# The products for v in blocks of 256 features over both halves of a third, with their split weights kept in DRAM

## The chip, the cores and the metric

The kernel runs on one core of a Trainium2 chip. The metric is the device time of one execution in microseconds (us), as the median of several runs. Five engines work beside each other, each through its own queue in program order: PE (TensorE, whose weight loads are listed apart as PEld), DVE (VectorE), ACT (ScalarE), POOL (GpSimd) and SP (SyncE), which issues nearly all DMA transfers here.

## The reference

One layer of a bidirectional encoder trunk on 1024 + 2048 positions of width 1024, all in float32. The change touches only the columns `v_a` of the input projection, which go through GELU and a layer norm over their 1024 features before the position mixing:

```python
h = rmsnorm(x, norm_g[i])
proj = h @ w_in[i]
u_a, v_a, z_a, x_b, z_b = jnp.split(proj, splits, axis=-1)
y_a = gmlp_branch(gelu(u_a), gelu(v_a), z_a, ...)   # u * (w_s mixes layernorm(v)) * silu(z)
y_b = s5_branch(x_b, z_b, ...)                      # two scans, GELU, GLU, silu(z)
x = x + jnp.concatenate([y_a, y_b], axis=-1) @ w_out[i]
return rmsnorm(x, final_g)
```

## The kernel before

**Split products.** Every float32 operand of a big product is held as two float32r parts, hi (index 0) and lo (index 1), and a product is three matmuls: hi by hi, hi by lo, lo by hi (`mm3`, L57 to L61). A weight piece of 1024 x 128 or 256 x 512 values is a tile `whl` (two parts, 1 MB together). `stage_next` lets SP load it from the input as two tiles `wf` of 128 x 512 (L107), of which there is one buffer each; `split_w` then makes hi on ACT (`S.copy`, L151) and lo on POOL (`G.tensor_tensor`, L152). Of `whl` there are two buffers. `next_w` does one `split_w` and one `stage_next`, after a sweep or part has used a tile.

**Thirds and stages.** The 3072 rows are three thirds, each of two halves (`jh`) of 512 rows, each half of four chunks of 128 rows. A half's normalised and transposed input is eight tiles `ha0..7` or `hb0..7` (two parts, 128 features x 512 rows). Phase one makes x_b for all thirds (0 to 398 us). Phase two (398 to 1824 us) takes the thirds in the order 2, 0, 1; each has a **v stage**, a **z stage** (zb, with the position mixing `mix`, whose products go to tiles `sv`) and a **u stage** (u and za). In z and u a weight piece is the stationary operand of 24 matmuls for each half, 48 in all (`sweep`). The last phase does the GLU and the output projection.

**The v stage.** Here the chunk of h is stationary and 512 features of the weights stream. The loops run over `jh`, two blocks `cb` of 512 features and four quarters `q` of the 1024 inputs: 16 weight pieces in a third, each used for one half only, in 24 matmuls (L494 to L496, four chunks, each with a PSUM bank `acc`). At the last quarter ACT applies GELU (L499). After the first half `half_stats(0)` takes bn_stats, bn_aggr and an inverse square root by Newton steps (`newton_rsqrt`, L48 to L53) on DVE, and `norm_chunk` and `split_chunk` prepare the first chunk for `mix`.

**Kept weights.** In the first third run, the split tiles of z, u and za (24) are also written to DRAM (`wc_d`, L154); the other two thirds read them back ready-made (L146), without ACT and POOL. The v pieces are loaded and split anew in each third.

**Side work.** `advance` is called at the same points as `next_w` and a few more; it advances 64 groups of state-space scans (`s5_groups`) through phase two: matmuls `pb` and `py`, and on DVE a chain of products, two scans and products (L1068 to L1086). Names of S5 tiles are `b`, `h`, `u`, `gt`, `tab`. For the second and third third `get_half` loads the tiles `ha`, `hb` back from DRAM (`hf<-hs_d`, L417) through the two buffers of `stage_tile` and splits them (L421 on ACT, L422 on POOL and DVE by turns). The scheduler orders each engine's instructions by the priorities given (`tc.high_priority`).

Of the kernel before, what the change touches and what calls it, by code (L numbers as in the profile page):

```python
# [11 lines left out]
F32 = mybir.dt.float32  # L12
# [3 lines left out]
AF = mybir.ActivationFunctionType  # L16
# [5 lines left out]
P = 128  # L22
D = 1024
KT = 8
# [7 lines left out]
HP = 100  # L32
# [31 lines left out]
def hybrid_encoder(ctx, tc, a, outs):  # L64
# [19 lines left out]
    wc_d = dram.tile([3 * KT, P, 2 * KT * P], F32, name="wc_d")  # L84
# [30 lines left out]
    def load_wv(col, q):  # L115

        src = w_in[256 * q:256 * q + 256, col:col + 512].rearrange("(kt p) c -> p kt c", p=P)
        return ([stage_w(i, src[:, i:i + 1]) for i in range(2)],
                lambda w: w.rearrange("p s (t a) c -> p s t (a c)", t=2))
# [6 lines left out]
    for i in range(NTH):  # L126
        order += [(None, load_wv, D + 512 * cb, q) for _ in range(2) for cb in range(2) for q in range(4)]
        feats = [4 * D + P * fb for fb in range(KT)] + [2 * D * z + P * fb for fb in range(KT) for z in range(2)]
        order += [(n, load_w, f) if i == 0 else (n,) for n, f in enumerate(feats)]
# [233 lines left out]
    with ExitStack() as p2:  # L363
# [64 lines left out]
        for th in (2, 0, 1):  # L428
# [3 lines left out]
            lns = {}  # L432

            def half_stats(jh):

                with tc.high_priority(offset=HP):
                    mv = small.tile([P, 4, 2], F32, tag="mv", name="mv")
                    for c in range(4):
                        st = small.tile([P, 2, 6], F32, tag="st", name="st")
                        for i in range(2):  # L440
                            V.bn_stats(st[:, i], vs[jh][:, c, 512 * i:512 * i + 512])
                        V.bn_aggr(mv[:, c], st)
                    ve = small.tile([P, 4], F32, tag="ve", name="ve")
                    V.tensor_scalar(ve, mv[:, :, 1], EPS, None, op0=ALU.add)
                    rs = newton_rsqrt(nc, small, ve, 4, "rv")
                    nb = small.tile([P, 4], F32, tag="nb", name="nb")
# [37 lines left out]
            for jh in range(2):  # L484
                for cb in range(2):
                    acc = [ps_mm.tile([P, 512], F32, tag="mm", name="acc") for _ in range(4)]
                    for q in range(4):
                        w = ready.pop(0)
                        for c in range(4):
                            csl = slice(P * c, P * c + P)  # L490
                            for i in range(2):
                                h = hs[jh][2 * q + i]
                                first, last = q == 0 and i == 0, q == 3 and i == 1
# [648 lines left out]
```

## Time and profile before

| what | value |
|---|---|
| runs: median (lowest to highest of 3) | 2626.35 us (2624.52 to 2627.77) |
| profiled execution: own time / span of its trace | 2629.88 / 2628.0 us |
| mean granted clock of PE in the profile | 0.979 |
| PE busy / PEld | 2472.4 us (94%) / 2033.7 us (77%) |
| DVE / ACT / POOL busy | 1812.0 (69%) / 1041.8 (40%) / 745.6 us (28%) |

Busy time is the union of an engine's instructions in the span. A matmul's listed length includes its way through the array, so what a matmul costs in a dense row is read from start to start. The granted clock is a share of full speed: 1.0 is 2.4 GHz and 0.5 is 1.2 GHz.

### The profile page before, as it was taken

The page shows a single profiled execution, that of the slowest core. Times are in us where ns is not written, and L with a number is a line of the kernel's source. Part 1 is how long each engine was busy: PE and PEld are TensorE (multiplying, and loading weights), DVE is VectorE, ACT ScalarE, POOL GpSimd, SP SyncE. Part 2 cuts the span into 40 slices and gives each one's busy share as a digit, 9 for nine tenths or more (in the row PEclk, how much of TensorE's full clock was granted, in tenths as well). Part 3 has the DMA queues.
Part 4 walks back from the last instruction along what each step waited for, and adds up shares of the span by engine and source line. Part 5 has one row for each costly group of instructions (what it writes and reads, how often), then busy time and mean ns, then how long its engine had stood idle before and what let it go on. Part 6 is the DMA issues. An engine that isn't in the chain of part 4 may idle for free.

```text
span 2628.0 us, 32080 instructions
## 1 busy us (share of the span) xinstructions
PE 2472.4 (94%) x11161; PEld 2033.7 (77%) x11161; DVE 1812.0 (69%) x2890; ACT 1041.8 (40%) x1809; POOL 745.6 (28%) x703
## 2 busy tenths in 40 slices
PE   6899998898998789999988899999999999999998
PEld 5777786777877677888877778887888888888887
DVE  6897857898988898888888998883443443333332
ACT  5343344455445455554445545433232321111110
POOL 1579865544323463211135421101000100000000
PEclk9999998999999899999999999999999999999999
DMA  8565453344554534444444334445565642222221
GB/s 231 172 193 156 131 148 112 110 155 142 173 169 145 172 102 129 130 137 147 132 142 123 110 126 141 133 141 180 168 172 163 198 151 97 96 97 97 92 73 36
DMA packets 369028, 362.90 MB, mean 138 GB/s; under 512 B 41665, under 2 KB 305377, under 8 KB 359649
## 3 DMA queue, kind: packets, MB, share of 16 engines
q1 hardware_dynamic: 317024, 339.80, 41.3%
q10 hardware_dynamic: 51840, 21.04, 3.2%
q8 instruction: 88, 1.44, 0.2%
q14 instruction: 76, 0.61, 0.1%
HBM read 233.95 MB, written 126.81 MB: 137 GB/s over the span
## 4 chain that ended last, share of the span: by engine, by line
PE 44%; DVE 27%; issue 6%; ACT 6%; POOL 5%; DMA 4%; SPq 0%; ACTq 0%; POOLq 0%; DVEq 0%
PE mm L59 13%; PE mm L61 13%; PE mm L60 13%; DVE gt L1078 6%; POOL whl L152 2%; DVE h L1084 1%; DVE h L1083 1%; DVE b L1070 1%; DVE b L1069 1%; DVE h L1086 1%; DVE b L1071 1%; DVE tab L1028 1%; DVE u L1017 1%; DVE b L1068 1%; DVE v L543 1%
## 5 line engine op out<-in xcount | busy, mean ns | idle before, releaser
L152 POOL TENSOR_TENSOR whl<-wf,whl 128x512 fp32r<-128x512 f32 x192 | 295.8, 1558 | 300.4 <-ACT whl L151 274.9
L61 PE MATMUL mm<-w,yh 128*128 128x512 f32 x768 | 301.4, 393 | 0.0
L60 PE MATMUL mm<-w,yh 128*128 128x512 f32 x768 | 301.1, 392 | 0.0
L59 PE MATMUL mm<-w,yh 128*128 128x512 f32 x768 | 301.1, 392 | 0.0
L59 PE MATMUL mm<-ha,whl 128*128 128x512 f32 x704 | 282.3, 401 | 18.5 <-ACT whl L151 11.2
L61 PE MATMUL mm<-ha,whl 128*128 128x512 f32 x704 | 279.2, 397 | 2.3 <-POOL whl L152 2.1
L60 PE MATMUL mm<-ha,whl 128*128 128x512 f32 x704 | 279.0, 396 | 0.0
L59 PE MATMUL mm<-hb,whl 128*128 128x512 f32 x704 | 276.8, 393 | 0.0
L60 PE MATMUL mm<-hb,whl 128*128 128x512 f32 x704 | 275.0, 391 | 0.0
L61 PE MATMUL mm<-hb,whl 128*128 128x512 f32 x704 | 274.6, 390 | 0.0
L1078 DVE TENSOR_TENSOR_SCAN gt<-dec,b 64x768 f32<-64x768 f32 x128 | 239.5, 1871 | 3.7
L59 PEld LDWEIGHTS mm<-ha,whl 128*128 128x128 f32 x704 | 134.9, 192 | 47.6 <-ACT whl L151 12.6
L60 PEld LDWEIGHTS mm<-w,yh 128*128 128x128 f32 x768 | 144.2, 188 | 32.9
L59 PEld LDWEIGHTS mm<-w,yh 128*128 128x128 f32 x768 | 144.2, 188 | 32.6
L61 PEld LDWEIGHTS mm<-w,yh 128*128 128x128 f32 x768 | 144.1, 188 | 32.5
L1073 ACT ACTIVATE dec<-keep,r 128x768 f32<-128x768 f32 x64 | 60.1, 939 | 275.3 <-DVE gt L1078 275.3
L661 DVE SCALAR_TENSOR_TENSOR yh<-yf,yh 128x512 fp32r<-128x512 f32 x96 | 66.9, 699 | 146.4 <-ACT yh L660 109.2
L151 ACT CAST whl<-wf 128x512 fp32r<-128x512 f32 x192 | 112.5, 618 | 127.0 <-DMA wf<-in_w_in_dram 36.3
L61 PEld LDWEIGHTS mm<-ha,whl 128*128 128x128 f32 x704 | 134.8, 191 | 34.2 <-POOL whl L152 5.4
L690 DVE TENSOR_TENSOR xr<-xr,mm 128x512 f32<-128x512 f32 x48 | 33.0, 688 | 182.9 <-PE mm L61 182.9
L1017 POOL TENSOR_TENSOR mo<-m,mo 128x384 fp32r<-128x384 f32 x64 | 79.1, 1237 | 278.1 <-ACT mo L1016 265.4
L60 PEld LDWEIGHTS mm<-ha,whl 128*128 128x128 f32 x704 | 135.2, 192 | 26.7 <-DVE ha L285 0.4
(242 smaller groups left out, 5759.0 us busy)
## 6 DMA issues: line engine op xcount, KB each, us to landing
wf<-in_w_in_dram SPq DMA_DIRECT2D x192, 256.0 KB
whl<-wc_d SPq DMA_DIRECT2D x48, 1024.0 KB
wc_d<-whl SPq DMA_DIRECT2D x24, 1024.0 KB
m<-mat_d SPq DMA_DIRECT2D x128, 128.0 KB
xb_d<-xo SPq DMA_DIRECT2D x24, 512.0 KB
U<-xb_d SPq DMA_DIRECT2D x64, 192.0 KB
gy_d<-gy SPq DMA_DIRECT2D x64, 192.0 KB
zb_d<-zb SPq DMA_DIRECT2D x24, 512.0 KB
```

What stands on the lines that cost most here:

```text
L59: nc.tensor.matmul(out, lh, rh, start=first, stop=False)
L60: nc.tensor.matmul(out, lh, rl, start=False, stop=False)
L61: nc.tensor.matmul(out, ll, rh, start=False, stop=last)
L151: S.copy(flat[:, 0, sl], wf)
L152: G.tensor_tensor(flat[:, 1, sl], wf, flat[:, 0, sl].bitcast(F32), op=ALU.subtract)
L543: V.scalar_tensor_tensor(t, t, LG[:, fb:fb + 1], RB[:, fb:fb + 1].to_broadcast([P, 4, P]), op0=ALU.mult, op1=ALU.add)
L661: V.scalar_tensor_tensor(y[:, 1], yf, sc, y[:, 0].bitcast(F32), op0=ALU.mult, op1=ALU.subtract)
L690: V.tensor_tensor(x, x, t.ps[i], op=ALU.add)
L1017: eng.tensor_tensor(t[:, 1], src, t[:, 0].bitcast(F32), op=ALU.subtract)
L1028: V.scalar_tensor_tensor(fr, kio, f8l[:, g + q:g + q + 1], fr, op0=ALU.mult, op1=ALU.add)
L1073: S.activation(dec.rearrange("p (i k) -> p i k", i=2), keep.unsqueeze(1).to_broadcast(sh), AF.Copy, scale=r8[:, g:g + 1])
L1078: V.tensor_tensor_scan(o[r, f], dec[r, f], bf[r, f], 0.0, op0=ALU.mult, op1=ALU.add)
```

## The change

The v stage handles blocks of 256 features for both halves of a third. A weight piece is now 512 inputs x 256 features; a third has 8 instead of 16, each used for both halves, in 2 x 48 matmuls of 256 columns. Two chunks share a PSUM bank, so a block holds four banks for its eight chunks. Four parts `v_part` (half, input half `q`) make a block; the first block takes both of the first half's parts first. bn_stats is issued as soon as 512 features of a chunk are there. `half_stats(0)` and the first chunk's norm and split now stand before the last part of the last block. The v pieces, too, are written to `wc_d` in the first third run and read back in the others (8 + 24 tiles instead of 24).

```diff
-    wc_d = dram.tile([3 * KT, P, 2 * KT * P], F32, name="wc_d")
+    wc_d = dram.tile([4 * KT, P, 2 * KT * P], F32, name="wc_d")
...
     def load_wv(col, q):
 
-        src = w_in[256 * q:256 * q + 256, col:col + 512].rearrange("(kt p) c -> p kt c", p=P)
-        return ([stage_w(i, src[:, i:i + 1]) for i in range(2)],
-                lambda w: w.rearrange("p s (t a) c -> p s t (a c)", t=2))
+        src = w_in[512 * q:512 * q + 512, col:col + 256].rearrange("(kt p) c -> p kt c", p=P)
+        return [stage_w(i, src[:, 2 * i:2 * i + 2]) for i in range(2)], lambda w: w
...
-        order += [(None, load_wv, D + 512 * cb, q) for _ in range(2) for cb in range(2) for q in range(4)]
-        feats = [4 * D + P * fb for fb in range(KT)] + [2 * D * z + P * fb for fb in range(KT) for z in range(2)]
-        order += [(n, load_w, f) if i == 0 else (n,) for n, f in enumerate(feats)]
+        todo = [(load_wv, D + 256 * cb, q) for cb in range(4) for q in range(2)]
+        todo += [(load_w, 4 * D + P * fb) for fb in range(KT)]
+        todo += [(load_w, 2 * D * z + P * fb) for fb in range(KT) for z in range(2)]
+        order += [(n, *f) if i == 0 else (n,) for n, f in enumerate(todo)]
...
-            for jh in range(2):
-                for cb in range(2):
-                    acc = [ps_mm.tile([P, 512], F32, tag="mm", name="acc") for _ in range(4)]
-                    for q in range(4):
...
+            def v_part(acc, w, cb, q, jh):
+
+                for cc in range(2):
+                    ps = acc[jh][cc]
+                    for i in range(2):
+                        csl = slice(P * (2 * cc + i), P * (2 * cc + i) + P)
+                        for t in range(4):
+                            h, wh, wl = hs[jh][4 * q + t], w[:, 0, 2 * t:2 * t + 2], w[:, 1, 2 * t:2 * t + 2]
+
+                            mm3(nc, ps[:, i], h[:, 0, csl], h[:, 1, csl], wh, wl, q == t == i == 0, q == i == 1 and t == 3)
+                    if q:
+                        c = slice(2 * cc, 2 * cc + 2)
+                        sl = slice(256 * cb, 256 * cb + 256)
+                        with tc.high_priority(offset=HP):
+                            S.activation(vs[jh][:, c, sl], ps, AF.Gelu_apprx_tanh)
+                            for i in (2 * cc, 2 * cc + 1) if cb % 2 else ():
+                                V.bn_stats(sts[jh][:, i, cb // 2], vs[jh][:, i, 512 * (cb // 2):256 * cb + 256])
+                advance()
+
+            for cb in range(4):
+                acc = [[ps_mm.tile([P, 2, 256], F32, tag="mm", name="acc") for _ in range(2)] for _ in range(2)]
+                ws = [ready.pop(0) for _ in range(2)]
+
+                for jh, q in ((0, 0), (0, 1), (1, 0), (1, 1)) if cb == 0 else ((0, 0), (1, 0), (0, 1), (1, 1)):
+                    v_part(acc, ws[q], cb, q, jh)
+                    if jh:
+                        next_w()
+                    if cb == 3 and (jh, q) == (0, 1):
+                        half_stats(0)
+                        norm_chunk(0)
+                        split_chunk(0, 0)
+                        split_chunk(0, 1)
```

The new file's lines are 7 higher from `s5_groups` on (its L1068 is now L1075), and lines of the v stage moved by a few.

On PE, at the start of the second v stage, the rows before are these (`ha_8178`, `ha_8181` are the first two input tiles of the half):

```order
L494 MATMUL acc<-whl,ha_8178 128x512
L495 MATMUL acc<-whl,ha_8178 128x512
L496 MATMUL acc<-whl,ha_8178 128x512
L494 MATMUL acc<-whl,ha_8181 128x512
L495 MATMUL acc<-whl,ha_8181 128x512
L496 MATMUL acc<-whl,ha_8181 128x512
```

There they now are (`ha_8488` to `ha_8499` are the first four input tiles):

```order
L59 MATMUL acc<-whl,ha_8488 128x256
L60 MATMUL acc<-whl,ha_8488 128x256
L61 MATMUL acc<-whl,ha_8488 128x256
L59 MATMUL acc<-whl,ha_8491 128x256
L60 MATMUL acc<-whl,ha_8491 128x256
L61 MATMUL acc<-whl,ha_8491 128x256
L59 MATMUL acc<-whl,ha_8496 128x256
L60 MATMUL acc<-whl,ha_8496 128x256
L61 MATMUL acc<-whl,ha_8496 128x256
L59 MATMUL acc<-whl,ha_8499 128x256
L60 MATMUL acc<-whl,ha_8499 128x256
L61 MATMUL acc<-whl,ha_8499 128x256
```

The columns are halved, the count is doubled, and the first chunk already needs four input tiles instead of two.

On SP, where the second v stage begins, before (`hf` are the reloaded input tiles of the third, two feature blocks each; the first of the eight stands a few rows ahead; `wf` are v weights to be split; `ya_d<-za` is the last store of the third before):

```order
L417 DMA hf_8184<-hs_d 128x2x512
L107 DMA wf<-in_w_in_dram 128x512 x2
L417 DMA hf_8192<-hs_d 128x2x512
L417 DMA hf_8200<-hs_d 128x2x512
L515 DMA ya_d<-za 128x8x128
L107 DMA wf<-in_w_in_dram 128x512 x2
L1046 DMA m_8535<-mat_d 128x256
L417 DMA hf_8296<-hs_d 128x2x512
L417 DMA hf_8304<-hs_d 128x2x512
```

and now (`hf_8486` is the first of the eight):

```order
L417 DMA hf_8486<-hs_d 128x2x512
L1106 DMA gy_d<-gy 8x16x384
L1051 DMA m_8878<-mat_d 128x256
L1049 DMA U<-xb_d 128x1x384
L417 DMA hf_8494<-hs_d 128x2x512
L146 DMA whl<-wc_d 128x2048
L417 DMA hf_8502<-hs_d 128x2x512
L146 DMA whl<-wc_d 128x2048
L1053 DMA m_8880<-mat_d 128x256
L417 DMA hf_8510<-hs_d 128x2x512
L522 DMA ya_d<-za 128x8x128
L1055 DMA m_8880<-ks_d 128x1x128
```

The first two ready-made v tiles are read between the second, third and fourth input tile; the other four input tiles still follow the store.

On DVE, in the first third run, `half_stats(0)` ended like this before (the Newton steps L51 to L53 come three times; `v_4334` is v of the first half):

```order
L444 TENSOR_SCALAR ve<-mv 128x4
L48 TENSOR_SCALAR rvy<-ve 128x4
L51 TENSOR_TENSOR rva<-rvy 128x4
L52 SCALAR_TENSOR_TENSOR rva<-rva,ve 128x4
L53 SCALAR_TENSOR_TENSOR rvy<-rva,rvy 128x4
...
L447 SCALAR_TENSOR_TENSOR nb<-mv,rvy 128x4
L458 TENSOR_SCALAR v_4334<-v_4334,rvy,nb 128x1024 x4
```

and ends like this now (`v_4336` and `v_4337` are v of the first and second half):

```order
L53 SCALAR_TENSOR_TENSOR rvy<-rva,rvy 128x4
L498 BN_STATS st<-v_4337 128x6
L51 TENSOR_TENSOR rva<-rvy 128x4
L1086 MEMSET gt 64x2x2 x2
L52 SCALAR_TENSOR_TENSOR rva<-rva,ve 128x4
L440 BN_AGGR mv<-st 128x2
L1090 TENSOR_TENSOR h_5528<-gt,tab 128x768
L53 SCALAR_TENSOR_TENSOR rvy<-rva,rvy 128x4
L1091 TENSOR_TENSOR h_5529<-gt,tab 128x768
L445 SCALAR_TENSOR_TENSOR nb<-mv,rvy 128x4
L1024 TENSOR_TENSOR u<-U,u 128x384
L456 TENSOR_SCALAR v_4336<-v_4336,rvy,nb 128x1024
```

The small steps are now mixed with the second half's bn_stats and with one piece of an S5 group (L1075 to L1091 there, its two scans and its first four products included), and they stand at the end of the v stage instead of in its middle.

## Rows read from the trace of the kernel before

**Rows 1.** page, part 5: line, engine, op, tiles | busy us, mean ns | idle before

```profile
L152 POOL TENSOR_TENSOR whl<-wf,whl 128x512 fp32r<-128x512 f32 x192 | 295.8, 1558 | 300.4 <-ACT whl L151 274.9
...
L151 ACT CAST whl<-wf 128x512 fp32r<-128x512 f32 x192 | 112.5, 618 | 127.0 <-DMA wf<-in_w_in_dram 36.3
```

**Rows 2.** windows of the v stages: length, busy us (count) PE PEld DVE ACT POOL, clock

```profile
398.30:521.60 123.30, 108.60 (x449) 87.13 (x449) 99.76 (x116) 58.46 (x96) 68.66 (x46) 0.93 0.37 105
...
888.30:1025.00 136.70, 117.02 (x460) 91.47 (x459) 119.29 (x139) 71.38 (x115) 73.96 (x50) 0.90 0.41 124
...
1364.40:1495.70 131.30, 112.96 (x461) 89.11 (x460) 121.72 (x137) 65.97 (x112) 76.75 (x52) 0.94 0.43 126
```

**Rows 3.** waits of PE: who waited for whom: us in total, times, longest

```profile
PE acc L495 <- POOL whl L152: 30.5, 32, 2.1
...
PE mm L59 <- DMA whl<-wc_d: 1.9, 1, 1.9
```

**Rows 4.** waits of the DMA queue of SP, same columns

```profile
SPq L107 <- POOL whl L152: 398.4, 163, 10.1
```

**Rows 5.** timeline of PE, 414:435 us: start, length, line, op, tiles

```profile
414.89 0.63 PE L496 MATMUL acc<-whl,ha 128*128 128x512 f32 x1
...
420.64 0.40 PE L494 MATMUL acc<-whl,ha 128*128 128x512 f32 x1
...
422.74 0.34 PE L59 MATMUL pb<-u,mi 128*128 128x384 f32 x1
...
423.61 0.34 PE L61 MATMUL pb<-u,mi 128*128 128x384 f32 x1
...
425.17 0.39 PE L494 MATMUL acc<-whl,ha 128*128 128x512 f32 x1
...
434.46 0.40 PE L496 MATMUL acc<-whl,ha 128*128 128x512 f32 x1
```

**Rows 6.** timeline of weight loads, 522:535 us

```profile
528.76 0.19 PEld L477 LDWEIGHTS sv<-wsT,vh 128*128 128x128 f32 x1
...
529.33 0.19 PEld L478 LDWEIGHTS sv<-wsT,vh 128*128 128x128 f32 x1
```

**Rows 7.** timeline of PE, 522:535 us

```profile
528.82 0.33 PE L477 MATMUL sv<-wsT,vh 128*128 128x256 f32 x1
...
528.99 0.22 PE L478 MATMUL sv<-wsT,vh 128*128 128x128 f32 x1
```

**Rows 8.** timeline of DVE at the starts of v stages two and three

```profile
899.77 1.63 DVE L1070 TENSOR_TENSOR b<-b,b 128x384 f32<-128x384 f32 x1
...
910.27 0.68 DVE L422 TENSOR_TENSOR ha<-hf,ha 128x512 fp32r<-128x512 f32 x1
...
924.23 1.10 DVE L422 TENSOR_TENSOR hb<-hf,hb 128x512 fp32r<-128x512 f32 x1
...
1378.56 1.42 DVE L422 TENSOR_TENSOR ha<-hf,ha 128x512 fp32r<-128x512 f32 x1 [0.28 <-ACT ha L421]
...
1398.43 0.68 DVE L422 TENSOR_TENSOR hb<-hf,hb 128x512 fp32r<-128x512 f32 x1
```

**Rows 9.** timeline of POOL, 895:930 us

```profile
897.59 3.40 POOL L152 TENSOR_TENSOR whl<-wf,whl 128x512 fp32r<-128x512 f32 x2
```

**Rows 10.** timeline of DVE, 440:475 us, inside the first v stage

```profile
444.60 0.95 DVE L1068 TENSOR_TENSOR b<-pb,tab 128x768 f32<-128x768 f32 x1
...
446.44 0.56 DVE L1070 TENSOR_TENSOR b<-b,b 128x384 f32<-128x384 f32 x1
...
453.74 1.48 DVE L1084 TENSOR_TENSOR h<-gt,tab 128x768 f32<-128x768 f32 x1
...
458.25 1.27 DVE L441 BATCH_NORM_STATS2 st<-v 128x6 f32<-128x512 f32 x2
...
463.32 1.02 DVE L444 TENSOR_SCALAR ve<-mv 128x4 f32<-128x4 f32 x1
...
467.32 3.97 DVE L458 TENSOR_SCALAR v<-v,rvy,nb 128x1024 f32<-128x1024 f32 x4
```

More of the change, by code (lines that the diff above doesn't have):

```diff
@@ L432, in hybrid_encoder @@
             lns = {}
+            sts = [small.tile([P, 4, 2, 6], F32, tag=f"st{jh}", name="st", bufs=1) for jh in range(2)]
             def half_stats(jh):
                 with tc.high_priority(offset=HP):
-                    mv = small.tile([P, 4, 2], F32, tag="mv", name="mv")
+                    mv = small.tile([P, 4, 2], F32, tag="mv", name="mv", bufs=2)
                     for c in range(4):
[L439 to L443, printed above, removed]
+                        V.bn_aggr(mv[:, c], sts[jh][:, c])
+                    ve = small.tile([P, 4], F32, tag="ve", name="ve", bufs=2)
                     V.tensor_scalar(ve, mv[:, :, 1], EPS, None, op0=ALU.add)
                     rs = newton_rsqrt(nc, small, ve, 4, "rv")
-                    nb = small.tile([P, 4], F32, tag="nb", name="nb")
+                    nb = small.tile([P, 4], F32, tag="nb", name="nb", bufs=2)
                     V.scalar_tensor_tensor(nb, mv[:, :, 0], -1.0, rs, op0=ALU.mult, op1=ALU.mult)
@@ L482, in mix @@
                         V.tensor_tensor(o, o, sv[:, :, 1], op=ALU.add)
-            for jh in range(2):
-                for cb in range(2):
-                    acc = [ps_mm.tile([P, 512], F32, tag="mm", name="acc") for _ in range(4)]
-                    for q in range(4):
[L488 to L493, printed above, removed]
-                                T.matmul(acc[c], h[:, 0, csl], w[:, 0, i], start=first, stop=False)
-                                T.matmul(acc[c], h[:, 0, csl], w[:, 1, i], start=False, stop=False)
-                                T.matmul(acc[c], h[:, 1, csl], w[:, 0, i], start=False, stop=last)
-                            if q == 3:
-                                with tc.high_priority(offset=HP):
-                                    S.activation(vs[jh][:, c, 512 * cb:512 * cb + 512], acc[c], AF.Gelu_apprx_tanh)
-                        next_w()
-                        advance()
-                if not jh:
-                    half_stats(0)
-                    norm_chunk(0)
-                    split_chunk(0, 0)
-                    split_chunk(0, 1)
```

## The prediction

> **What bounds the kernel now.** I began with the busy shares: PE is busy 94% of the span, so time is won only where PE idles, runs at the lower clock or does less. Next I read PE's waits; the largest is that of the v products for POOL's lo part of a weight piece, 30.5 us in 32 waits [rows 3]. So I cut out the three v stages [rows 2]: 123.3, 136.7 and 131.3 us, 391.3 together. What would they take at full speed? In a dense row of PE the matmuls of 512 columns start every 0.2266 us (41 steps from 425.17 to 434.46), those of 384 columns every 0.174 us (5 steps from 422.74 to 423.61) [rows 5]. The windows count 449, 460 and 461 matmuls; 384 of each are v products, the rest (65, 76, 77) belong to S5. That makes 98.3, 100.2 and 100.4 us, 298.9 together. **92.4 us are lost in the v stages**, a little over half of it in listed idle time, the rest at the lower clock and in refilling the array. After such waits the v products from 414.89 to 420.64 took 5.75 us for 13 steps [rows 5] where full speed gives 2.95: one clock episode costs 2.8 us.
>
> The reason stands in the loop that makes a piece. A piece lasts 24 x 0.2266 = 5.4 us, but the next `wf` can be loaded only when POOL has released its single buffer: two passes of 1558 ns [rows 1], then a load, then ACT's pass of 618 ns. SP waited 398.4 us, 163 times, for exactly this release [rows 4]. The stages ran at 123.3/16 = 7.7 to 136.7/16 = 8.5 us a piece: they are paced by making pieces, not by PE.
>
> **The change, part by part.**
>
> *Pieces.* In the first third run 8 pieces are split instead of 16, in the others none instead of 32. 40 pieces fewer are 80 passes on each of two engines: 124.6 us of POOL and 49.4 us of ACT [rows 1], both off the path once PE does not wait. A piece now lasts 2 x 48 x 0.121 = 11.6 us (price below), longer than the 7.7 to 8.5 us that making one took. Ready-made pieces are read as z and u read theirs; those 48 reads cost PE one wait of 1.9 us [rows 3] with pieces that last 48 x 0.2266 = 10.9 us. So the whole loss of 92.4 us goes, except at the places named below. The bytes read stay near the same: 8 reads of 1 MB against 16 of 0.5 MB in a third; the 8 extra writes come in the first, beside a DMA share of 0.37 [rows 2].
>
> *Products.* 1152 matmuls of 512 columns become 2304 of 256. No dense row of 256 columns exists. From 512 to 384 columns a matmul loses 0.0526 us, so 256 should cost 0.2266 - 0.1052 = 0.121 us: 278.8 us against 261.0, **+17.8**. The lower bound is the weight load: beside the mixing products the loads follow each other every 0.114 us (5 steps from 528.76 to 529.33) [rows 6], which would give 262.7, +1.7. The upper bound is the 256-column product there, 0.17 us from its start to the next one's [rows 7], +130.7. I take 0.121: the products of 256 and 128 columns there take two load steps together, 0.23, so the 0.17 looks like a wait for loads, shared out unevenly.
>
> The page "TensorE: Matmul & The Clock Gate" of the Trainium skill, section "Back-to-back issue gap", speaks against halving columns: each matmul has a fixed share that the smaller one pays twice. It lists 518 and 262 cycles for 512 and 256 columns, which gives by my estimate 251.5 us against 248.6, +2.9 us. The trace's 0.2266 us is 544 cycles at 2.4 GHz, so its fixed share is larger, and I keep the rows.
>
> *The first block of the second and third third.* Before, the second half's input was needed only after two blocks of the first half. Now the first block needs all sixteen input tiles. A part takes 48 x 0.121 = 5.8 us; with 15 S5 products between (2.6 us) the block should end 25.8 us after the stage's start, its last part beginning at about 20. Before, DVE finished the last `hb` tile at 925.3, 37.0 us after the start at 888.3, and at 1399.1, 34.7 us after 1364.4 [rows 8, 2]. If that stayed, the block would end at 42.8 and 40.5, a loss of 17.0 and 14.7. But between those rows DVE and POOL were in each other's way: L1070 took 1.63 us beside a v split on POOL [rows 8, 9] and 0.56 us without one [rows 10], and those splits are gone. I take 5 us off each: **+21.7**, and two clock episodes, **+5.6**. Bounds: 0, if tiles come early enough, and 31.7 with the episodes on top. The last `ha` tiles, at +22.6 and +15.6 [rows 8], are wanted at +7; waiting for them uses the same time, since the last `hb` tile decides.
>
> On this contention the page "SBUF — State Buffer" of the Trainium skill, section "Who interferes with whom", says that a DVE instruction with two SBUF inputs and a GpSimd instruction that reads SBUF block each other. The trace agrees (1.63 against 0.56 us).
>
> *The first block of the first third.* The third piece can be split once the third part is done, and is wanted one part (about 7 us) later; ACT and POOL need 0.6 + 3.1 us [rows 1]. +2, between 0 and 6.
>
> *The turn to z.* `half_stats(0)` was in mid-stage, under cover of the second half's products. Now only one part covers it, and the first mixing product waits for its end. In the order of the new program PE has 15 S5 products, 48 v products and 24 of zb between: 2.6 + 5.8 + 5.4 = 13.8 us. DVE and ACT have, in a row: GELU and a cast, near 0.6 each like the cast of the same size [rows 1]; two bn_stats 1.3; one S5 piece from L1068 to L1084, 10.6 (444.60 to 455.22); four more bn_stats 2.5; the small steps 4.0 (463.32 to 467.32); a norm 1.0 [rows 10]. Together 20.6, so PE waits 6.8; with POOL quieter I take 6. Three times, with a clock episode each: **+18 + 8.4**. Bounds: 0, if DVE gets through earlier, and 12 each, if it comes half an S5 piece late. What waits behind PE's wait is the z sweep and S5's next products.
>
> *Nothing else.* GELU passes, bn_stats and S5 stay the same in number; bn_stats moves forward within the stage, on an engine that is busy for 93% of a stage at most [rows 2].
>
> Sum: -92.4 + 17.8 + 2 + 27.3 + 26.4 = -18.9 us. Against the profiled execution's own 2629.9 that is 2611.0; the median of the runs shown lies 3.5 lower, so **2607 us**.
>
> **The rivals.**
> - *The starts and turns are hidden.* If the input tiles come early and DVE reaches the norm in time, both terms vanish, and the kernel comes to 2626 - 72.6 = 2554; with one of the two hidden, about 2580. For it: POOL and ACT are much emptier there. Against it: the eight input tiles pass through two buffers, and one is held until the late store of za.
> - *DVE becomes the pace.* It is busy 340.8 us in the v stages, 93% in the last [rows 2]. If its work stayed and it could not exceed 93%, the stages would take 340.8 / 0.927 = 367.6 us; with the turn's 26.4 they are where they were, 394 against 391.3: 2629, no change. Against it: part of that busy time is the contention with the splits that go.
> - *The 256-column product costs more than it should.* At 0.17 us the kernel takes 2607 + 112.9 = 2720, slower. It decides from 0.129 us on, where the 18.9 us are eaten. For it stand only the uneven starts of rows 7; against it the two load steps for two products.
> - *The reads of pieces queue behind the input tiles.* The first two stand between them in SP's order, and the third follows the store of za. If each start lost 17 us more than I took, the kernel would end at 2641.
>
> **How the numbers follow.** My forecast (2595 to 2619, from the bounds of starts and turns halfway) gets 0.47. Hidden starts or turns 0.21 (2554 to 2595). DVE as the pace 0.14, between 2617 and 2633. The dear product 0.10, the queued reads 0.08. A measurement of this kernel can tell about 0.2% from no change, 5 us: faster is below 2621, slower above 2632. Faster 0.47 + 0.21 + 0.02 = 0.70, same 0.12, slower 0.18. The range 2572 to 2634 leaves out the far ends of the first rival, and the last two: less than 2 in 10.
>
> **What would show it.** Right: no waits of v products for L151 or L152 worth telling; v products 0.121 us apart; the first blocks of the second and third v stage some 10 us longer than the 26 us; a wait of about 6 us at the first `sv` of each z stage; POOL busy near 620 us. Wrong: product steps of 0.13 us or more; waits spread over the whole v stage (then DVE or SP has become the pace); no wait at all at the turns.

## The result and the profile after

The changed kernel took **2588.24 us** in the median of 4 runs (2584.94 to 2589.81), the kernel before beside it 2627.06 us (2624.52 to 2628.22): a ratio of 0.9852, with a 95% interval from 0.9835 to 0.9869. It is 38.8 us faster, where 18.9 us were forecast; the time lies inside the range of 2572 to 2634, but below the 2595 to 2619 that the forecast itself was given: it falls into the band of the rival of hidden starts or turns.

Page of the changed kernel, parts 1 and 5 (as in [rows 1]):

```profile
PE 2463.7 (95%) x12313; PEld 2089.4 (81%) x12313; DVE 1743.2 (67%) x2890; ACT 999.9 (39%) x1729; POOL 606.7 (23%) x623
...
L152 POOL TENSOR_TENSOR whl<-wf,whl 128x512 fp32r<-128x512 f32 x112 | 165.5, 1495 | 219.3 <-ACT whl L151 196.6
```

Windows of the v and z stages of the changed kernel, third by third; columns as in [rows 2], with the DMA share and GB/s last:

```profile
398.10:501.30 103.20, 103.20 (x834) 103.20 (x833) 83.57 (x109) 48.05 (x78) 36.42 (x28) 1.00 0.53 180
501.30:643.20 141.90, 124.86 (x591) 107.06 (x590) 130.10 (x187) 77.92 (x140) 59.26 (x43) 0.94 0.44 142
...
874.50:992.20 117.70, 109.65 (x844) 107.87 (x845) 88.58 (x118) 52.12 (x81) 19.31 (x17) 0.97 0.42 136
992.20:1121.20 129.00, 121.11 (x596) 104.77 (x595) 113.57 (x188) 69.29 (x124) 34.98 (x28) 0.97 0.39 126
...
1338.80:1452.20 113.40, 108.72 (x845) 107.61 (x844) 89.48 (x130) 50.04 (x82) 21.69 (x18) 0.97 0.44 144
1452.20:1579.20 127.00, 119.56 (x588) 103.07 (x587) 112.31 (x176) 63.69 (x116) 32.84 (x27) 0.97 0.40 126
```

The z stages of the kernel before, in the same view:

```profile
521.60:657.70 136.10, 122.50 (x590) 105.25 (x589) 122.12 (x179) 76.34 (x138) 57.22 (x41) 0.96 0.47 155
...
1025.00:1147.50 122.50, 119.09 (x596) 102.92 (x595) 107.91 (x174) 67.93 (x123) 30.73 (x26) 0.99 0.42 133
...
1495.70:1622.00 126.30, 116.91 (x586) 100.52 (x585) 109.33 (x169) 64.29 (x116) 30.31 (x25) 1.00 0.40 129
```

The v stages went from 391.3 us [rows 2] to 103.2 + 117.7 + 113.4 = 334.3 us, **57.0 less**. The z stages went from 384.9 to 397.9 us, **13.0 more**, in the parts 5.8, 6.5 and 0.7. The u stages stayed: 646.4 us in the same windows before, 646.1 now. With 1.2 us more between stages and 2.0 us more outside phase two, that is the 41.1 us between the two profiled spans (2628.0 and 2586.9 us). DVE is busy 261.6 us in the v stages where it was 340.8, POOL 77.4 where it was 219.4 [rows 2].

The waits of PE, groups of the v products and the mixing products `sv`, first one row of the kernel before, then the changed kernel:

```profile
PE sv L477 <- DVE zb L512: 20.5, 13, 2.6
```

```profile
PE sv L475 <- DVE zb L519: 19.8, 9, 3.3
...
PE acc L59 <- ACT ha L421: 7.8, 2, 4.8
...
PE sv L475 <- ACT vh L463: 6.8, 2, 4.9
...
PE sv L476 <- POOL vh L464: 1.5, 1, 1.5
...
PE acc L59 <- DMA whl<-wc_d: 1.7, 2, 1.2
```

The 30.5 us of v products behind POOL [rows 3] are gone, and no wait of `acc` for L151 or L152 is left. What waits in the v stages now are `acc` products for input tiles, mostly `ha`, as the prediction had it.

The waits of `sv` products for `zb` (mixing products that wait until DVE has drained a z product) are not what grew: 20.5 us in 13 waits before, 19.8 us in 9 now. New are the 6.8 and 1.5 us for `vh`, the split first chunk, at the turns. PE's idle time in the three z stages, length less busy time, went from 26.4 to 32.4 us, 6.0 more. The other 7.0 us of the 13.0 are PE's busy time, 365.5 us where it was 358.5, with three products more and a lower granted clock in each stage (0.94, 0.97, 0.97 where it was 0.96, 0.99, 1.00).

The timeline of PE has the steps of a dense row, and the first `sv` product of each z stage:

```profile
399.16 0.28 PE L61 MATMUL acc<-whl,ha 128*128 128x256 f32 x1
...
402.62 0.28 PE L60 MATMUL acc<-whl,ha 128*128 128x256 f32 x1
...
513.56 0.79 PE L475 MATMUL sv<-wsT,vh 128*128 128x256 f32 x2 [4.93 <-ACT vh L463]
...
1001.19 0.39 PE L475 MATMUL sv<-wsT,vh 128*128 128x256 f32 x1 [1.83 <-ACT vh L463]
...
1458.73 0.28 PE L475 MATMUL sv<-wsT,vh 128*128 128x256 f32 x1
```

From 399.16 to 402.62 are 29 steps, 0.1193 us each. The whole first v stage confirms it: 834 products, 66 of them S5's at 0.174 us, leave 91.7 us for 768, **0.1194 us** each. With it the second v stage's products (768, and 76 of S5) need 104.9 us and the third's (77 of S5) 105.1: they lost 12.8 and 8.3 us. Windows of the first block of each v stage:

```profile
398.10:422.26 24.16, 24.16 (x201) 24.16 (x199) 16.51 (x19) 8.93 (x15) 8.85 (x8) 1.00 0.67 219
874.49:914.21 39.72, 31.67 (x216) 29.89 (x217) 28.10 (x31) 17.72 (x28) 11.36 (x9) 0.91 0.53 173
1338.84:1372.68 33.84, 29.16 (x209) 28.05 (x208) 26.69 (x33) 14.94 (x27) 12.73 (x10) 0.90 0.62 201
```

Of the 216 products of the second row 24 are S5's, of those of the third 15 (two more reach over the window's edge). At 0.1194 and 0.174 us that is 27.1 and 25.5 us: the first blocks lost 12.6 and 8.3 us, so nearly all that the stages lost.

### The profile page after: what moved, and what is told of

Same layout as the page of the kernel before. It is cut to its first block, busy times and chain, and to the rows that moved or that the text cites. A ratio compares the mean times of both kernels' runs of the same rounds, so it can differ in the third digit from the quotient of the medians.

```text
span 2586.9 us, 34044 instructions
## 1 busy us (share of the span) xinstructions
PE 2463.7 (95%) x12313; PEld 2089.4 (81%) x12313; DVE 1743.2 (67%) x2890; ACT 999.9 (39%) x1729; POOL 606.7 (23%) x623
## 4 chain that ended last, share of the span: by engine, by line
PE 58%; DVE 19%; issue 3%; ACT 3%; DMA 3%; POOL 1%; SPq 0%; DVEq 0%; ACTq 0%; POOLq 0%
PE mm L59 15%; PE mm L61 15%; PE mm L60 15%; DVE gt L1085 4%; PE acc L61 3%; PE acc L59 3%; PE acc L60 3%; DMA hf<-hs_d 1%; DVE h L1090 1%; DVE b L1076 1%; DVE h L1091 1%; DVE v L550 1%; DVE b L1075 1%; DVE b L1077 1%; DVE tab L1035 1%
## 5 line engine op out<-in xcount | busy, mean ns | idle before, releaser
L1085 DVE TENSOR_TENSOR_SCAN gt<-dec,b 64x768 f32<-64x768 f32 x128 | 232.9, 1820 | 3.8
L152 POOL TENSOR_TENSOR whl<-wf,whl 128x512 fp32r<-128x512 f32 x112 | 165.5, 1495 | 219.3 <-ACT whl L151 196.6
L61 PEld LDWEIGHTS mm<-hb,whl 128*128 128x128 f32 x704 | 133.6, 190 | 28.1
```

What stands on the lines that cost most here:

```text
L61: nc.tensor.matmul(out, ll, rh, start=False, stop=last)
L152: G.tensor_tensor(flat[:, 1, sl], wf, flat[:, 0, sl].bitcast(F32), op=ALU.subtract)
L1085: V.tensor_tensor_scan(o[r, f], dec[r, f], bf[r, f], 0.0, op0=ALU.mult, op1=ALU.add)
```

## Experiments

All times are medians of four or five runs beside nine runs of the kernel before. The ratios' intervals are about 0.0013 to either side, 3.5 us.

| kernel | median us | ratio to before |
|---|---|---|
| v pieces split anew | 2595.94 | 0.9882 |
| old blocks, pieces kept | 2587.50 | 0.9852 |
| last block in the first block's order | 2587.13 | 0.9854 |
| more buffers for input tiles | 2581.34 | 0.9825 |
| first block in the others' order | 2591.83 | 0.9861 |
| first half's norms on ACT | 2579.75 | 0.9818 |
| blocks of 256 in the first third alone | 2576.28 | 0.9803 |
| buffers + norms | 2574.83 | 0.9796 |
| order + norms | 2583.31 | 0.9832 |
| buffers + order + norms | 2577.31 | 0.9812 |
| buffers + all norms on ACT | 2578.76 | 0.9808 |
| buffers + norms, S5 moved from z to v | 2587.63 | 0.9837 |

**1. Which part of the change brings the gain?** First the reuse alone:

```diff
-        order += [(n, *f) if i == 0 else (n,) for n, f in enumerate(todo)]
+        order += [(n if n >= KT else None, *f) if i == 0 or n < KT else (n,) for n, f in enumerate(todo)]
```

> The changed kernel with one part undone: the v pieces are not kept, each of the eight of a third is loaded and split anew in the second and third third too. My theory: what paced the v stages was that a piece served only one half, 5.4 us of products against 7.7 to 8.5 us of making; with both halves it lasts 11.6 us, so PE should hardly wait for L151 or L152 although 16 pieces more are split. The first blocks would lose what the prediction had before its deduction of 5 us each, some 17 and 15 us, as POOL and DVE are in each other's way again: v stages two and three of about 122 and 120 us against 117.7 and 113.4, the kernel near 2598 us (2592 to 2604). Rival: the gain of the second and third v stage comes from keeping the pieces, thus from the splits that go from ACT and POOL; then these stages fall back to about 130 us each and the kernel to about 2617 us.

Measured 2595.94 us, as my theory had it. Windows of its second and third v stage:

```profile
869.70:992.40 122.70, 111.46 (x844) 109.66 (x844) 101.16 (x123) 61.44 (x98) 44.11 (x32) 0.94 0.35 105
1338.30:1459.20 120.90, 110.64 (x845) 109.32 (x844) 103.43 (x128) 57.95 (x98) 50.45 (x34) 0.96 0.35 103
```

With the reuse alone the kernel is 31.6 us faster than the kernel before beside it; a piece that serves both halves hardly needs keeping. What keeping adds is 5.0 us in the second v stage and 7.5 us in the third, where POOL is busy 19.3 and 21.7 us instead of 44.1 and 50.4, and DVE 12.6 and 13.9 us less with nearly as many instructions (118 and 130, here 123 and 128). The prediction had deducted 5 us a start for the quieter POOL. The run does not separate that from the 16 passes each that ACT and POOL have to fit in here, but DVE's slowing shows in single rows of the second v stage, first of the changed kernel, then of this run:

```profile
L1077 DVE TENSOR_TENSOR b<-b,b 128x384 f32<-128x384 f32 x6 | 3.3, 556 | 0.2
```

```profile
L1077 DVE TENSOR_TENSOR b<-b,b 128x384 f32<-128x384 f32 x6 | 4.5, 755 | 0.2
```

L1075, which has one of its two inputs in PSUM (`pb`), takes 952 ns in both.

Then keeping alone:

```diff
-    wc_d = dram.tile([3 * KT, P, 2 * KT * P], F32, name="wc_d")
+    wc_d = dram.tile([5 * KT, P, 2 * KT * P], F32, name="wc_d")
...
-        order += [(None, load_wv, D + 512 * cb, q) for _ in range(2) for cb in range(2) for q in range(4)]
...
+        todo = [(load_wv, D + 512 * cb, q) for _ in range(2) for cb in range(2) for q in range(4)]
...
+        order += [(n, *f) if i == 0 else (n,) for n, f in enumerate(todo)]
```

> The kernel before with the other part alone: blocks of 512 features and one half, 16 pieces a third as before, but the 16 split pieces are kept in DRAM in the first third run and read back in the others. My theory: the first v stage stays at 123 us or gets a little longer; in the other two a piece lasts 5.4 us, and a read of 1 MB took 5.9 and 7.7 us from its issue to the matmul that waited for it at the start of the changed kernel's second v stage, so PE still waits at many pieces, but less: stages of 16 x 6 to 7.5 us with S5, 105 to 125 us against 136.7 and 131.3; the kernel between 2585 and 2612 us, I say 2597. Rival: the reads keep up, both stages come to 100 to 105 us, and the kernel to 2562 to 2570 us, faster than with the whole change, so that the halved products and the reuse would be a loss there.

Measured 2587.50 us, as fast as the whole change. Windows of v and z in the second third and of v in the third, and then the row of PE's waits for the reads:

```profile
889.70:1004.60 114.90, 106.87 (x459) 88.07 (x460) 97.89 (x136) 53.45 (x84) 23.48 (x19) 0.96 0.61 212
1004.60:1127.40 122.80, 120.40 (x596) 104.23 (x595) 107.70 (x172) 67.01 (x121) 31.41 (x26) 0.97 0.42 133
1343.30:1453.90 110.60, 104.89 (x461) 87.20 (x461) 97.36 (x137) 49.46 (x81) 25.82 (x20) 0.97 0.65 221
```

```profile
PE acc L496 <- DMA whl<-wc_d: 15.1, 8, 4.3
```

The first v stage stayed at 122.5 us. In the others the reads nearly keep up (15.1 us of waits in 32 reads), and since half_stats stays in mid-stage, the z stages stay near their old lengths, 137.3, 122.8 and 125.5 us. So two ways lead out of the same loop: making pieces faster, or using each longer. The whole change gains in the first third what it gives away in the others.

That calls for a kernel with each third in its better form:

```diff
+            if th == 2:
+                for cb in range(4):
...
+            else:
+                for jh in range(2):
+                    for cb in range(2):
+                        acc = [ps_mm.tile([P, 512], F32, tag="mm", name="acc") for _ in range(4)]
+                        for q in range(4):
```

> The first third run has the changed v stage (blocks of 256 features, both halves, eight pieces split); its pieces are written to DRAM in the shape of the old blocks, and the other two thirds run the old v stage (512 features, one half, half_stats in mid-stage) on 16 reads of these. My theory: the two ways against the loss are each enough in a v stage, so each third can take the one that costs it least: first third as in the changed kernel (103.1 and 141.9 us for v and z), the others as in the run that only kept the pieces (115.0, 122.7, 110.6, 125.5 against 117.7, 129.0, 113.4, 127.0): 13 us less than the changed kernel, about 2575 us (2570 to 2580). Rival: the reads are slowed or late in another place, since the pieces are written in four parts each, and the waits for reads grow: 2580 to 2595 us.

Measured 2576.28 us, where 2575 was expected: the two parts add by stages.

**2. What holds the first blocks?**

```diff
+                    if kt % 4:
+                        two = [wpool.tile([P, 512], F32, tag=f"wf{i}", name="hw", bufs=1) for i in range(2)]
+                        for i in range(2):
+                            dma(two[i], hs_d[hf, kt + i])
```

> The changed kernel, but every second pair of reloaded input tiles goes through the two wf buffers, which nothing uses there, instead of the two shared with zb and za: three loads of 512 KB under way instead of at most two. My theory: the first blocks of the second and third v stage wait for input tiles whose loads wait for a buffer (ACT sat idle 5.8 us until a load had landed, just before PE's longest wait of 4.8 us there); with more buffers the loss of 11.6 and 7.3 us in these stages falls to about a half, and the kernel to about 2579 us (2574 to 2584). Rival: the splits of the sixteen tiles on ACT, POOL and DVE between S5's work set the time, or the transfers take the time of the DMA engines; then nothing changes, 2586 to 2590 us.

Measured 2581.34 us, 7 us less than the changed kernel. Windows of its second and third v stage, and then the row of PE's waits for v pieces:

```profile
876.40:983.10 106.70, 106.70 (x843) 106.70 (x844) 86.01 (x117) 50.03 (x76) 16.83 (x15) 0.98 0.42 140
1330.10:1443.60 113.50, 108.11 (x844) 107.83 (x845) 88.60 (x127) 50.39 (x80) 21.45 (x17) 0.97 0.40 130
```

```profile
PE acc L59 <- DMA whl<-wc_d: 10.4, 3, 5.4
```

In the second v stage the loss went from 12.8 to about 2 us, so the input tiles' two buffers had caused it; the stage began 2.6 us later behind the u stage, waiting for its first piece. In the third the loss stayed, with another cause: no input tile is waited for, but the first pieces are (10.4 us in both stages, the longest wait 5.4 in the third). There the rival of the queued reads came true, in a small form. The other edit here:

```diff
-                for jh, q in ((0, 0), (0, 1), (1, 0), (1, 1)) if cb == 0 else ((0, 0), (1, 0), (0, 1), (1, 1)):
+                for jh, q in ((0, 0), (1, 0), (0, 1), (1, 1)):
```

> The changed kernel with the first block of each v stage in the order of the other blocks: the first half's second part comes after the second half's first. My theory: the first blocks of the second and third v stage wait for the input tiles as they arrive, first half before second; the second part now needs hb tiles that were ready some 26 us after the start, and two more parts follow: the block ends 5 to 6 us later in each, and the kernel comes to about 2599 us (2594 to 2604). Rival: the last hb tile decides in either order, 30 us after the start, and the order costs nothing: 2586 to 2590 us.

Measured 2591.83 us, between the two, and not told apart from the changed kernel. In the program as scheduled the second v stage kept the old order of parts, and in the first all tiles are there; so only the third could show a price: 116.1 us against 113.4. The forecast of 5 to 6 us is not borne out, but it was tested once only.

**3. What lengthens the z stages?**

```diff
-                for jh, q in ((0, 0), (0, 1), (1, 0), (1, 1)) if cb == 0 else ((0, 0), (1, 0), (0, 1), (1, 1)):
+                for jh, q in ((0, 0), (0, 1), (1, 0), (1, 1)) if cb in (0, 3) else ((0, 0), (1, 0), (0, 1), (1, 1)):
```

> The changed kernel with the last block of each v stage in the order of the first block, both parts of the first half first, so that half_stats(0), the first norm and its split have two parts of cover instead of one. My theory: the z stages grew by 5.8, 6.7 and 0.6 us because the first sv product waits for this chain (5.1, then 2.0 and 1.8 us, with the clock behind them); 5.8 us more of cover takes these waits away: z stages of 136, 123 and 126 us, the kernel near 2577 us (2573 to 2582). A cost of up to 2 us a third may come at the z stage's first piece, whose read or split can start only after the third part. Rival: the z stages grew because DVE carries the second half's bn_stats and an S5 piece into them whatever the order; then nothing changes, 2586 to 2590 us.

Measured 2587.13 us, the rival's number; its mechanism is not shown by that. (By the windows above the z stages had grown by 5.8, 6.5 and 0.7 us.) Windows of its z stages:

```profile
501.70:641.50 139.80, 124.17 (x590) 107.18 (x589) 123.78 (x181) 76.78 (x138) 59.46 (x45) 0.94 0.47 152
992.70:1119.50 126.80, 120.58 (x595) 104.54 (x595) 112.96 (x176) 68.16 (x123) 34.80 (x27) 0.97 0.41 129
1450.20:1577.00 126.80, 119.50 (x588) 103.07 (x587) 112.00 (x172) 65.31 (x116) 34.36 (x27) 0.97 0.40 127
```

The waits for `vh` at the turns were gone, but PE's idle time in the z stages fell only from 32.4 to 29.2 us: the later `sv` products waited 5.2 us longer for DVE than in the changed kernel (22.1 us instead of 19.8 for `zb`, 7.0 instead of 4.1 for `v`). So I took DVE's load for the cause, the norms above all:

```diff
-                    V.tensor_scalar(v, v, rs[:, q:q + 1], nb[:, q:q + 1], op0=ALU.mult, op1=ALU.add)
+                    if c < 4:
+                        S.activation(v, v, AF.Identity, scale=rs[:, q:q + 1], bias=nb[:, q:q + 1])
+                    else:
+                        V.tensor_scalar(v, v, rs[:, q:q + 1], nb[:, q:q + 1], op0=ALU.mult, op1=ALU.add)
```

> The changed kernel with the norms of the first half's four chunks (L456, one pass of 128 x 1024 each) on ACT instead of DVE; the second half's four stay on DVE. My theory now: the z stages grew by 5.8, 6.7 and 0.6 us because DVE, busy 92%, 88% and 88% of them, got work that it did in the v stages before: the norms of the first half, 23.5 us of L456 in the z stages against 9.0 before; taking the first wait away only moved it to later sv products that wait for zb on DVE. With these norms on ACT the z stages go back to what they were, about 136, 123 and 126 us, and the kernel to about 2576 us (2571 to 2581). Rival: the chain to the first sv product as such sets the loss (statistics, norm, split in a row); it is as long on ACT, and ACT's own queue of tables and GELU stands before it: 2585 to 2592 us.

Measured 2579.75 us, 8.5 us less, with z stages of 140.5, 127.4 and 122.7 us. The last fell by 4.3 us, the first two hardly. With the edit for the buffers as well:

> The changed kernel with both edits: more buffers for the reloaded input tiles, and the first half's norms on ACT. My theory: the two losses lie in different stages and add, 7 us from the buffers and about 12 us from the norms: about 2569 us (2563 to 2575). Rival: the norms on ACT change nothing, and this stays where the buffers alone were, 2579 to 2583 us.

Measured **2574.83 us** (2572.62 to 2575.92), a ratio of 0.9796 (0.9783 to 0.981), the least median of all runs, though not told apart from the 2576.28: 13.4 us less than the changed kernel, where 7 + 8.5 would be the sum. If the first wait and the load were the two causes, the edits for order and norms together had to bring the first z stage back, without the buffers and with them:

> The changed kernel with the last block in the first block's order and the first half's norms on ACT, the two edits for the turn to z together. My theory: a z stage now loses by either of two things, the first sv product that waits for the chain of statistics, norm and split, and DVE that has more to do than before; each edit alone takes one away and leaves the other (the order alone gave 139.8, 126.9 and 126.8 us for the z stages, the norms alone 140.5, 127.3 and 122.7). Together: about 136, 123 and 122 us and the kernel near 2572 us (2568 to 2576). Rival: the order buys nothing even then, since something else holds the z stages at these times: 2578 to 2582 us as with the norms alone.

> The changed kernel with the three edits together: more buffers for the reloaded input tiles, the last block in the first block's order, the first half's norms on ACT. My theory: 5 to 7 us less than the buffers and the norms together (2574.8 us), as the first waits of the z stages go and DVE has no more work there than in the kernel before: about 2568 us (2564 to 2572), the least of all. Rival: the order buys nothing: 2572 to 2576 us.

Measured 2583.31 and 2577.31 us, each a little more than without the order (2579.75 and 2574.83), though the intervals overlap. My theory fell. Window of the first z stage with order and norms together:

```profile
501.60:643.50 141.90, 124.99 (x591) 107.18 (x590) 120.69 (x176) 78.93 (x142) 61.39 (x46) 0.94 0.46 150
```

DVE is busy 120.7 us in it, less than before the change (122.1), and the stage still takes 141.9 us against 136.1. DVE's load does not set it alone. The last two runs start from the one with buffers and half the norms. They ask for the load once more, and for S5's place:

```diff
-                    if c < 4:
-                        S.activation(v, v, AF.Identity, scale=rs[:, q:q + 1], bias=nb[:, q:q + 1])
...
+                    S.activation(v, v, AF.Identity, scale=rs[:, q:q + 1], bias=nb[:, q:q + 1])
```

> The changed kernel with more buffers for the input tiles and now all eight norms of a third on ACT. The theory that DVE's work in the z stages alone sets their length has lost ground: with the order and the norms together DVE was busy 120.7 us in the first z stage, less than the 122.1 us before the change, and the stage still took 141.8 us against 136.1. If DVE's load counts all the same, four more norms of 0.8 to 1.4 us off it shorten each z stage by 2 to 4 us: about 2567 us (2563 to 2571). Rival: what counts is where S5's scans stand on DVE when a zb product waits to be drained, and ACT, which the norms now keep from the casts behind them, is no better: 2572 to 2580 us.

Measured 2578.76 us; the z stages were 142.4, 127.6 and 123.5 us long, with DVE 6.1, 3.2 and 2.9 us less busy than in the run with buffers and half the norms. The load is refuted as the one cause.

```diff
-                advance()
+                advance(0.5625)
...
-                sweep(ps_mm, lambda jh: hs[jh], [lambda *x: zb_op(fb, *x)], advance)
+                sweep(ps_mm, lambda jh: hs[jh], [lambda *x: zb_op(fb, *x)], lambda: advance(0.4375))
```

> The changed kernel with more buffers and the first half's norms on ACT (2574.8 us), and an eighth of the S5 work of each z stage moved to the v stage of the same third: 0.5625 a part there and 0.4375 a product here, 0.5 in both before. My theory now: the v stage used to be long enough for DVE to catch up with S5 (99.8 us busy in 123.3); at 103 us DVE is 81% busy there, enters the z stage with S5's work still queued and is 92% busy in it, so that zb's drains and the sv products behind them come late. Some 12 us of S5 moved from z to v even this out: DVE near 92% in the first v stage and 84% in its z stage, z stages shorter by 4 to 6 us beyond the 2 us that the moved S5 products take, v stages longer by the 2 us of these: about 2562 us (2556 to 2569). Rival: the waits at the zb drains are of one S5 piece standing ahead and do not go with the load, or the v stages begin to wait for S5: 2572 to 2582 us.

Measured 2587.63 us, 12.8 us worse than without this edit; most of that lies elsewhere, in the second v stage (116.2 us instead of 107.7, behind a late piece) and the first u stage (231.8 instead of 226.8). The run tells something on the z stages all the same. Windows of its first and third z stage, and then from its timeline of DVE the turn to the third (L448 and L451 are the changed kernel's L442 and L445, L1094 its L1085):

```profile
503.00:636.20 133.20, 121.39 (x581) 104.59 (x580) 115.67 (x177) 76.64 (x135) 59.66 (x43) 0.95 0.45 142
...
1444.20:1577.60 133.40, 122.47 (x581) 105.39 (x580) 110.13 (x184) 67.12 (x120) 32.27 (x26) 0.94 0.37 119
```

```profile
1444.05 0.16 DVE L448 TENSOR_SCALAR ve<-mv 128x4 f32<-128x4 f32 x1
...
1448.43 1.69 DVE L1094 TENSOR_TENSOR_SCAN gt<-dec,b 64x768 f32<-64x768 f32 x1
...
1451.54 1.75 DVE L1094 TENSOR_TENSOR_SCAN gt<-dec,b 64x768 f32<-64x768 f32 x1
...
1454.31 0.11 DVE L451 SCALAR_TENSOR_TENSOR nb<-mv,rvy 128x4 f32<-128x4 f32 x1
```

The first z stage became 8.7 us shorter and the third 11.3 us longer than in the run with the same buffers and norms (141.9 and 122.1), each with fewer products of PE (581 against 590 and 588). In the first DVE had 10.8 us less to do, which alone could explain it; in the third it was 2.3 us busier, which could not. What changed there is where S5's pieces stand: two scans now lie inside the small steps of half_stats, which take 10.3 us from `ve` to `nb`. In the third z stage PE then waits 5.5 us for `vh` instead of 0.3 and is busy 5.8 us longer at the lower clock (0.94 instead of 1.00), which is nearly the whole 11.3 us. In the changed kernel's timeline of DVE the same steps of the first and third turn, and a drain of `zb` in mid-stage, are these:

```profile
498.68 0.16 DVE L442 TENSOR_SCALAR ve<-mv 128x4 f32<-128x4 f32 x1
...
501.21 1.74 DVE L1085 TENSOR_TENSOR_SCAN gt<-dec,b 64x768 f32<-64x768 f32 x1
...
504.10 2.81 DVE L1085 TENSOR_TENSOR_SCAN gt<-dec,b 64x768 f32<-64x768 f32 x1
...
511.36 0.15 DVE L445 SCALAR_TENSOR_TENSOR nb<-mv,rvy 128x4 f32<-128x4 f32 x1
...
1449.47 0.16 DVE L442 TENSOR_SCALAR ve<-mv 128x4 f32<-128x4 f32 x1
...
1452.83 0.16 DVE L445 SCALAR_TENSOR_TENSOR nb<-mv,rvy 128x4 f32<-128x4 f32 x1
...
1484.54 3.54 DVE L1085 TENSOR_TENSOR_SCAN gt<-dec,b 64x768 f32<-64x768 f32 x2
...
1490.10 0.68 DVE L519 SCALAR_TENSOR_TENSOR zb<-zb,mm 128x512 f32<-128x512 f32 x1
```

and on PE, the `sv` product behind that drain, with the window of the six us from there:

```profile
1490.83 0.39 PE L475 MATMUL sv<-wsT,vh 128*128 128x256 f32 x1 [3.13 <-DVE zb L519]
```

```profile
1490.20:1496.20 6.00, 5.37 (x21) 4.83 (x22) 5.99 (x10) 4.44 (x9) 1.41 (x1) 0.72 0.30 87
```

The first turn takes 12.7 us from `ve` to `nb`, with two scans in between, and PE waits 4.93 us at 513.56. The third takes 3.4 us, with none, and PE does not wait. The drain at 1490.10 stands behind two scans and two products, and the next `sv` product, at 1490.83, had waited 3.13 us for it; behind it the granted clock fell. The third z stage of the kernel before had waits for `zb` of the same sum, 7.4 us, and kept a clock of 1.00; why it fell here is not shown.

So in these turns the steps take long where S5's scans stand among them. The last run's first turn shows that this is not the whole cost (DVE, then PE):

```profile
504.21 0.16 DVE L448 TENSOR_SCALAR ve<-mv 128x4 f32<-128x4 f32 x1
...
507.56 0.16 DVE L451 SCALAR_TENSOR_TENSOR nb<-mv,rvy 128x4 f32<-128x4 f32 x1
```

```profile
513.92 0.39 PE L484 MATMUL sv<-wsT,vh 128*128 128x256 f32 x1 [4.25 <-ACT vh L472]
```

Its steps take 3.4 us with no scan among them, but they begin 1.2 us after the stage's start (503.0), where the changed kernel's begin 2.6 us before it: S5's products stand ahead of them. PE still waits 4.25 us. Most of this stage's 8.7 us were therefore not won at the turn, but behind it: 2.1 us of waits for `zb` instead of 6.2, and PE 4.5 us less busy.

## Why the prediction came out as it did

It was right in its direction and in what gives the gain. The terms that it set against the gain were too large, the one for the turns above all, so the time came out below the forecast's own band, in that of the rival of hidden starts or turns; only the third turn was hidden in the way that rival meant. Of its own signs all came but one: the wait of about 6 us at the first `sv` came in the first turn alone. By its own steps:

- **The lost 92.4 us** went, except at the places it named: -92.4 + 14.1 (products) + 21.1 (stages two and three, 12.8 + 8.3) = -57.2, against 57.0 measured. This sum closes by construction, since the losses are what the stages took beyond their products; that they lie at the first blocks is shown by the windows of these (12.6 and 8.3). That the loop of making pieces paced the stages is shown twice, by the run with reuse alone and by that with keeping alone.
- **Products.** The step from 512 and 384 columns down to 256 gave 0.121 us; measured 0.1194. 2304 x 0.1194 - 261.0 = +14.1 instead of +17.8. Neither the load step of 0.114 [rows 6] nor the 0.17 of [rows 7] was the price, though the weight loader was busy throughout, so what sets the 0.1194 is not shown. By the 262 cycles that the Trainium skill lists (page "TensorE: Matmul & The Clock Gate", section "Back-to-back issue gap") it would, by my estimate, have been 0.109 us at 2.4 GHz; the trace has 287 cycles, and the measurement decides.
- **The first block of the first third:** +2 forecast, nothing lost.
- **The first blocks of the others:** 27.3 forecast, 20.9 measured. They ended 39.7 and 33.8 us after the start, where 37.8 and 35.5 were used; the sum is right. The two clock episodes on top (5.6) were too much: the last tile sets the block's end, and a slow PE ahead of it loses nothing more, though the granted clock did fall (0.91 and 0.90). The other 0.8 us is work that is not lost: nine S5 products more than I had counted there, less what the v products were cheaper. The deduction for a quieter POOL fits the split-anew run, whose stages took 5.0 and 7.5 us longer, though not all of that need be the contention. The Trainium skill (page "SBUF — State Buffer", section "Who interferes with whom") says that a DVE instruction with two SBUF inputs contends with a GpSimd instruction that reads SBUF. The trace agrees: L1077, with two such inputs, took 755 ns in the stage with the splits and 556 ns in the one without them.
- **The turn to z is the term that was furthest off:** "Three times, with a clock episode each", +26.4; measured +13.0. Of its two parts the waits were mis-sized: 18 us forecast, and 8.3 us measured at the turns (4.93 in the first, 1.83 and 1.53 in the second, none in the third), of which 2.3 us were won back at other waits of the z stages. I had put one S5 piece into each turn's chain. It stands so in the first turn, partly in the second, and not in the third. The clock came near its price, 8.4 forecast and 7.0 us of longer busy time measured, but in part by luck: in the third stage it fell behind a drain of `zb` and not at the turn. The term was also built wrongly. It priced one wait, and the run in which this wait is gone had z stages only 2.1, 2.2 and 0.2 us shorter. And the step "Nothing else" did not list that the first half's norms move into the z stages; with these on ACT the third z stage fell by 4.3 us, the first two hardly.
- **The rivals.** DVE did not become the pace of the v stages: its busy time there fell to 261.6 us. The dear product did not occur. The queued reads cost 1.7 us, and 10.4 us where the input tiles were loaded earlier. The hidden starts and turns came true for the third turn alone.

Together 3.7 (products), 8.2 (starts, 2 + 27.3 against 21.1) and 13.4 us (turns) less than forecast, and 3.1 us more at stage edges and outside: the 22.2 us between -18.9 and the -41.1 us of the two spans.

Open is what exactly holds the first z stage near 140 us in all runs with the changed v stage but one. It was 133.2 us in the last run, which moved S5's place on DVE and its load together; no run fixes the place without moving something else.

## What to carry to other kernels

When a loop that makes operands is the pace, compare how long one operand is used with how long one takes to make. Using it longer and making it cheaper are then two remedies for one loss: the second one applied brings only what the first left. A chain moved to the end of a stage must be priced with what its engine's queue holds at that place in each pass, since a long side task that stands there in one pass may not stand there in the next. A wait that is taken away from the front of a busy stage can come back behind it, so such a gain is read from the stage's length and not from the wait.

## What the runs showed of the hardware

- A product of 256 columns costs 0.1194 us in a dense row beside weight loads for each. With one load to each product the weight loader was busy for all of the first v stage's 103.2 us, and PE still did not wait; the granted clock was 1.00 there, against 0.93 in the same stage before [rows 2].
- DVE's busy time rose with POOL's, by about half as much, in the one run that tests it: with 8 pieces split again in each of two v stages, POOL was 24.8 and 28.8 us busier in them, and DVE 12.6 and 13.9 us, with nearly as many instructions. L1077, with two inputs in SBUF, slowed from 556 to 755 ns in the one and from 580 to 665 ns in the other; L1075, with one of them in PSUM, took 952 to 954 ns in all four.
- Reads of 1 MB every 7 us, 16 in a row, nearly kept up in the run that only keeps the pieces: with the other transfers of the two v stages they moved 212 and 221 GB/s at a DMA share of 0.61 and 0.65, and left PE 15.1 us of waits.
